# A two-layer hybrid decoder step on one NeuronCore: first K tiles in smaller chunks, operand sums of the output projection later, two retention fetches one piece sooner

## Chip, cores and metric

The kernel runs on one core of one Trainium2 chip. The metric is device microseconds of one execution, as the median of several runs; lower is better.

## What is computed

Two layers run over 520 columns: 512 prompt tokens and 8 sample tokens that share all weights. Cut to what matters:

```
h = RMSNorm(x); z = h @ W_in                       # 2048 -> 8192
conv:       y_c = B * conv3(C * xc) * silu(g)       # 1024 wide
retention:  o_n = sum_{m<=n} gamma^(n-m) (R q_n . R k_m) v_m   # 4 heads of 256
            y_r = groupnorm(o) * silu(g_ret)
x = x + concat(y_c, y_r) @ W_out                    # output projection
x = x + sigmoid(x @ W_pg) * (p @ W_ple)             # gate projection
```

A final RMSNorm follows. Outputs are x for both groups, the last two rows of the convolution's input, and the retention state.

## The kernel before

Activations lie transposed, features on partitions: 16 tiles (K tiles) of 128 x 520. All large products are done in three fp32r matmuls (`mm3`, L245): every operand is split into a high part (ScalarE, ACT, a copy that rounds) and a low part (VectorE, DVE, source minus high). Weights stream in from DRAM by SyncE (SP) in pieces of up to 128 x 512 (`load`, L220), are split (`split_w`, L225: L229 on ACT, L230 on DVE) and are used once. The 520 columns are two halves of 260, so that a product of two row tiles with two column halves can be done with seven products in place of eight (`strassen`, L290), for the first s of 16 K tiles; s is given per row pair by tables such as OUT_ROWS, and 0 means `plain` (L270). The seven products need sums of operand halves, on the weights' side (L319) and on the activations' side.

Those activation operands belong to class `Operands` (L423). Its list `todo` has one entry per K pair: split it as plain operands, and (or) sum it. `build` does the first entry: `operand_sums` (L410) makes two sum tiles by four DVE instructions of 260 columns (L413 to L416), `split` (L545: L551 on ACT, L552 on DVE, L554 and L555 where a gain is applied) splits tiles, and the source tiles are freed. Entries are built where the program calls `fill` or `need`; `fill` builds while tiles of the pair are ready and enough of the 75 tile slots are free (7 beyond the reserve for a pair that is split and summed, 3 otherwise). The first four pairs are split and summed in one go; the other pairs are split, and later loaded again and summed. For the output projection (operands `O`, L1073) the rows are 0, 8, 16, 16, 16, 16, 16, 0: the first row pair is plain, the second uses sums of four K pairs, the third of eight. Its inputs are written during the stages before: `yc` by the convolution (L1112), `ys` by retention (L1000), and are fetched by POOL's DMA queue (L1058, L1063).

At the start (L675 to L708) there is no time to stream: the four row tiles of the first two pairs are computed at once, K tiles in chunks of 1, 3, 4, 4, 4. For a chunk, SP issues a weight load for each of the four row tiles and the chunk's input tiles between them, then all are split.

Retention of a head is cut into nine pieces s0 to s8 (L1007 to L1046), which are queued and done one at a time in the middle and at the end of later row pairs (`aside`). A head's q, k, v and gate are written to DRAM and fetched again by half (256 tokens, `fetch`, L866, on POOL's queue); `send(c, "vf")` fetches the values of half c, `"gf"` the gate. A piece takes what an earlier piece has fetched.

The program is written in this order, but the order in which each engine issues is made by a list scheduler when the kernel is built (only the tail of the last layer is kept as written). Each engine then issues strictly in its order and waits on semaphores.

## Time and profile before

| | |
|---|---|
| median of 3 runs | 2168.64 us (2165.82 to 2170.73) |
| the profiled execution | 2169.1 us, span of its instructions 2167.3 us |
| PE (TensorE) busy | 2147.8 us, 99% of the span, 17861 matmuls |
| DVE (VectorE) busy | 1896.1 us, 87% |
| ACT (ScalarE) busy | 1264.5 us, 58% |
| POOL busy | 430.6 us, 20% |
| DMA | 387.31 MB, mean 179 GB/s |
| granted TensorE clock | 0.999 of full speed |

Matmuls are pipelined: a row's length runs from start to end of one matmul, and the next one starts before that end. A bracket behind a row of the timeline gives the time that the engine sat idle just before it, and which instruction's end released it.

### The profile page before, as it was taken

How to read it: one execution, taken by the hardware profiler on the slowest of the kernel's cores; microseconds unless marked ns; L12 is line 12 of the kernel's file. 1: busy time of each engine (PE TensorE's matmuls, PEld its weight loads, DVE VectorE, ACT ScalarE, POOL GpSimd, SP SyncE). 2: the span in 40 equal slices, each digit the busy share in tenths (PEclk: the TensorE clock that was granted, in tenths of full speed). 3: DMA queues.
4: the chain of work that ended last, by engine and by line, in shares of the span. 5: the costliest groups of instructions: out<-in, count | busy, mean ns of one | idle time of the engine just before them, and what ended most of it. 6: DMA issues, size and time to landing. Idle time of an engine off the chain costs nothing. (4 is left out here: it accounts for less than half of the span.)

```text
span 2167.3 us, 48178 instructions
## 1 busy us (share of the span) xinstructions
PE 2147.8 (99%) x17861; PEld 2142.1 (99%) x17861; DVE 1896.1 (87%) x3849; ACT 1264.5 (58%) x2647; POOL 430.6 (20%) x746
## 2 busy tenths in 40 slices
PE   9999999999999999999999999999999999999998
PEld 9999999999999999999999999999999999999998
DVE  8889988998999987987997988989999998879884
ACT  8656655565555655655765655565645555456565
POOL 2313222211001211200212222231111022011011
PEclk9999999999999999999999999999999999999999
DMA  8555565545543745645645566664464355566455
GB/s 288 171 175 197 181 217 184 178 157 175 158 129 118 238 156 187 215 154 160 215 144 175 172 213 191 189 209 170 151 182 149 120 158 202 176 207 200 128 164 198
DMA packets 182861, 387.31 MB, mean 179 GB/s; under 512 B 25888, under 2 KB 56352, under 8 KB 182624
## 3 DMA queue, kind: packets, MB, share of 16 engines
q1 hardware_dynamic: 128704, 212.98, 31.6%
q0 software_dynamic: 53056, 169.84, 23.8%
q8 instruction: 140, 2.29, 0.4%
q10 hardware_dynamic: 864, 1.39, 0.2%
q14 instruction: 97, 0.79, 0.1%
HBM read 318.96 MB, written 65.15 MB: 177 GB/s over the span
## 5 line engine op out<-in xcount | busy, mean ns | idle before, releaser
L247 PE MATMUL ps_g<-slot,split 128*128 128x260 f32 x5465 | 1531.6, 284 | 7.2 <-ACT slot L307 2.9
L248 PE MATMUL ps_g<-slot,split 128*128 128x260 f32 x5465 | 1534.3, 282 | 0.3 <-DVE slot L555 0.3
L249 PE MATMUL ps_g<-slot,split 128*128 128x260 f32 x5461 | 1519.9, 283 | 0.5 <-DVE split L230 0.5
L229 ACT ACTIVATE split<-raw 128x512 fp32r<-128x512 f32 (+2 forms) x1347 | 777.3, 596 | 583.1 <-DVE raw L319 213.2
L247 PEld LDWEIGHTS ps_g<-slot,split 128*128 128x128 f32 x5465 | 1024.0, 188 | 10.1 <-ACT slot L307 3.7
L248 PEld LDWEIGHTS ps_g<-slot,split 128*128 128x128 f32 x5465 | 1028.5, 188 | 0.5 <-DVE slot L555 0.5
L249 PEld LDWEIGHTS ps_g<-slot,split 128*128 128x128 f32 x5461 | 1019.8, 188 | 1.0 <-DVE split L230 1.0
L230 DVE TENSOR_TENSOR split<-raw,split 128x512 fp32r<-128x512 f32 (+2 forms) x1346 | 849.2, 652 | 172.5 <-PE ps_g L248 85.4
L319 DVE TENSOR_TENSOR raw<-raw 128x512 f32<-128x512 f32 (+1 forms) x660 | 428.9, 660 | 32.5 <-DMA raw<-wi 23.7
L307 ACT ACTIVATE slot<-ps_g 128x260 f32<-128x260 f32 x336 | 127.4, 381 | 140.6 <-PE ps_g L249 122.7
L551 ACT ACTIVATE slot<-slot 128x520 fp32r<-128x520 f32 (+1 forms) x212 | 109.2, 562 | 46.6 <-DVE slot L414 11.1
L552 DVE TENSOR_TENSOR slot<-slot,slot 128x520 fp32r<-128x520 f32 (+1 forms) x212 | 124.4, 620 | 4.1 <-ACT slot L551 3.9
L781 POOL DMA_DIRECT2D o_rets<-slot x64 | 35.3, 552 | 351.6 <-DVE slot L780 131.7
L307 DVE TENSOR_TENSOR slot<-ps_g,slot 128x260 f32<-128x260 f32 x168 | 70.9, 424 | 6.0 <-PE ps_g L249 3.7
L869 POOL DMA_DIRECT2D slot<-hs x64 | 46.2, 724 | 118.7 <-DVE split L230 42.7
L814 POOL DMA_DIRECT2D hs<-slot x64 | 35.6, 556 | 139.3 <-DVE slot L755 61.3
L780 DVE SCALAR_TENSOR_TENSOR slot<-slot,vs,slot 128x256 f32<-128x256 f32 x128 | 56.1, 481 | 4.5 <-ACT slot L776 4.3
L746 DVE TENSOR_TENSOR slot<-slot,slot 128x520 f32<-128x520 f32 x80 | 55.8, 698 | 4.7 <-DMA o_rets<-slot 3.7
L770 POOL DMA_DIRECT2D slot<-sret x64 | 35.5, 554 | 114.6 <-ACT split L229 37.3
L1058 POOL DMA_DIRECT2D slot<-x1s x76 | 40.8, 538 | 87.6 <-PE ps_g L249 27.2
L1209 POOL DMA_DIRECT2D x2s<-slot x30 | 16.4, 545 | 201.6 <-DVE slot L1204 200.6
L771 POOL DMA_DIRECT2D slot<-kq x64 | 34.9, 547 | 106.0 <-DVE slot L876 22.2
(217 smaller groups left out, 1733.8 us busy)
## 6 DMA issues: line engine op xcount, KB each, us to landing
raw<-wi SPq DMA_DIRECT2D x377, 256.0 KB, 3.9
raw<-wo SPq DMA_DIRECT2D x128, 256.0 KB, 5.4
raw<-wg SPq DMA_DIRECT2D x122, 256.0 KB, 4.1
raw<-wi SPq DMA_DIRECT2D x136, 192.0 KB, 4.0
slot<-x1s POOLq DMA_DIRECT2D x76, 260.0 KB, 5.1
slot<-sret POOLq DMA_DIRECT2D x64, 256.0 KB, 4.0
hs<-slot POOLq DMA_DIRECT2D x64, 256.0 KB, 4.0
slot<-hs POOLq DMA_DIRECT2D x64, 256.0 KB, 5.2
```

What stands on the lines that cost most here:

```text
L229: S.activation(hi, raw, AF.Copy)
L230: V.tensor_tensor(lo, raw, F(hi), SUB)
L247: PE.matmul(out, wh, xh, start=start, stop=False, skip_group_check=more)
L248: PE.matmul(out, wh, xl, start=False, stop=False, skip_group_check=more)
L249: PE.matmul(out, wl, xh, start=False, stop=stop, skip_group_check=more)
L307: fn(*args)
L319: V.tensor_tensor(out[:, n], x[:, n], y[:, n], op)
L551: keep(S.activation(hi, src[:, n], AF.Copy))
L552: V.tensor_tensor(lo, src[:, n], F(hi), SUB)
L746: V.tensor_tensor(out[:, n], v, table[:, n], MUL)
L780: keep(V.scalar_tensor_tensor(st[:, c], k, vs[:, h, e, b : b + 1], st[:, c], MUL, ADD))
L869: SIDE.dma_start(t[:, :512].rearrange("p (m n) -> p m n", m=2), src)
```

## The change

It does three things. The start's second chunk (K tiles 1 to 3) becomes two, of one and two tiles. `Operands` gets `hold`: with hold 8 (output projection alone) no pair is summed when it is split; the source tiles of the first four pairs are kept in their slots, and are summed from there after all eight pairs have been split. In retention, the gate of the first half is fetched in s2 instead of s3, the values of the second half in s4 instead of s5.

```
--- before.py
+++ after.py
@@ -62,6 +62,7 @@
 RAW = 32
 WARM = 8
 FIRST = 8
+HOLD = (8, 0, 0)
 SPLIT = 60
 
 
@@ -423,13 +424,14 @@
     class Operands:
 
 
-        def __init__(self, rows, load, reserve=0, whole=False, gain=None):
+        def __init__(self, rows, load, reserve=0, whole=False, gain=None, hold=0):
             self.rows, self.load, self.reserve, self.whole, self.gain = rows, load, reserve, whole, gain
             self.sent = []
             self.ops = [None] * KT
             self.sums = []
             self.ready = 0
-            first = max(rows[0], min(FIRST, max(rows))) // 2
+            first = max(rows[0], 0 if hold else min(FIRST, max(rows))) // 2
+            self.held = {i: None for i in range(first, hold // 2)}
             self.todo = [(True, True)] * first + [(True, False)] * (KT // 2 - first)
             self.todo = [(i, *t) for i, t in enumerate(self.todo)]
             self.todo += [(i, False, True) for i in range(first, max(rows) // 2)]
@@ -440,21 +442,28 @@
 
         def send(self):
 
-            i = self.todo[len(self.sent)][0]
-            self.sent.append([self.load(k) for k in (2 * i, 2 * i + 1)])
+            i, plain, _ = self.todo[len(self.sent)]
+            if not plain and i in self.held:
+                self.sent.append(None)
+            else:
+                self.sent.append([self.load(k) for k in (2 * i, 2 * i + 1)])
 
         def build(self):
             if not self.sent:
                 self.send()
             i, plain, summed = self.todo.pop(0)
-            f = [self.ready_tile(k, t) for k, t in zip((2 * i, 2 * i + 1), self.sent.pop(0))]
+            f = self.sent.pop(0)
+            f = self.held[i] if f is None else [self.ready_tile(k, t) for k, t in zip((2 * i, 2 * i + 1), f)]
             if summed:
                 t = operand_sums(*f)
             if plain:
                 k = 2 * i
                 halves = not self.whole and k < max(self.rows)
-                self.ops[k] = split(f[0], halves=halves, right=not halves or self.right(k))
-                self.ops[k + 1] = split(f[1])
+                keeps = i in self.held
+                self.ops[k] = split(f[0], free_src=not keeps, halves=halves, right=not halves or self.right(k))
+                self.ops[k + 1] = split(f[1], free_src=not keeps)
+                if keeps:
+                    self.held[i] = f
             else:
                 put(*f)
             if summed:
@@ -670,9 +679,9 @@
     xs = []
     X = Operands(HEADS[0][2:] + CONVS[0], from_dram(xT), gain=lambda k: norm_g(0, k))
     X.todo = [t for t in ((i, False, True) for i in range(max(X.rows) // 2))]
-    X.ready = KT // 2
+    X.ready, X.held = KT // 2, {}
     rms = Rms()
-    for a, b in ((0, 1), (1, 4), (4, 8), (8, 12), (12, 16)):
+    for a, b in ((0, 1), (1, 2), (2, 4), (4, 8), (8, 12), (12, 16)):
         raws = []
         if b == 1:
             raw = raw_ring.get(4)
@@ -1016,22 +1025,22 @@
                 scores()
                 keys()
                 values(0)
+                send(0, "gf")
 
             def s3():
                 state(0)
                 within(0)
-                send(0, "gf")
                 send(1, "qf", "kf")
 
             def s4():
                 gate(0)
                 operands()
+                send(1, "vf")
 
             def s5():
                 carried()
                 scores()
                 keys()
-                send(1, "vf")
 
             def s6():
                 values(1)
@@ -1070,7 +1079,7 @@
                 return retained(k)
             return y.pop(k) if k in y else again(yc, k - 8)
 
-        O = Operands(OUT_ROWS[l], mixer, RESERVE_OUT)
+        O = Operands(OUT_ROWS[l], mixer, RESERVE_OUT, hold=HOLD[0])
 
         SIDE.dma_start(scv, sconv[l])
         S.activation(ncv[:, :, 2:18].rearrange("p j (b r) -> p j b r", r=2)[:, :, :, 0], scv[:, :, 1, :], AF.Copy)
@@ -1126,7 +1135,7 @@
         def gate_in(k):
             return x1.pop(k) if k in x1 else again(x1s, k)
 
-        Gt = Operands(GATES[l][: (KT - tail) // 2], gate_in, RESERVE_GATE, whole=bool(tail))
+        Gt = Operands(GATES[l][: (KT - tail) // 2], gate_in, RESERVE_GATE, whole=bool(tail), hold=HOLD[1])
         for m in range(0, KT, 2):
             xs = [get(), get()]
             for i in range(2):
@@ -1171,7 +1180,7 @@
 
         X = None
         if not tail:
-            X = Operands(HEADS[l + 1] + CONVS[l + 1], next_in, RESERVE_NEXT, gain=lambda k, l=l: norm_g(l + 1, k))
+            X = Operands(HEADS[l + 1] + CONVS[l + 1], next_in, RESERVE_NEXT, gain=lambda k, l=l: norm_g(l + 1, k), hold=HOLD[2])
         for m in range(0, KT - tail, 2):
             pes, xs = [], [again(x1s, m), again(x1s, m + 1)]
             later.append(lambda m=m, w=parts(wp[l, m // 2], 0, 4), pes=pes: embed(m, w, pes))
```

The lines of the changed kernel lie further down: L230 is there L231, L307 is L308, L413 to L416 are L414 to L417, L551 and L552 are L560 and L561, L869 is L878, L1112 is L1121.

How the built order moves, at three places of layer 0. First DVE, at the entry of the output projection, from one of the two adds that end the convolution's last row pair (a PSUM bank is read into a tile) to the other; L413 to L416 and L552 are the new projection's operands. Before:

```order
L307 TENSOR_TENSOR slot_464_9225<-ps_g,slot_464_9225 128x260
L414 TENSOR_TENSOR slot_491_9458<-slot_490_9374,slot_491_9458 128x260
L552 TENSOR_TENSOR slot_509_9504<-slot_507_9498,slot_509_9504 128x260
L230 TENSOR_TENSOR split<-raw,split 128x512
L552 TENSOR_TENSOR slot_510_9505<-slot_507_9498,slot_510_9505 128x260
L552 TENSOR_TENSOR slot_512_9511<-slot_508_9501,slot_511_9510 128x520
L552 TENSOR_TENSOR slot_496_9471<-slot_490_9374,slot_495_9470 128x520
L230 TENSOR_TENSOR split<-raw,split 128x512
L552 TENSOR_TENSOR slot_476_9340<-slot_468_9320,slot_475_9339 128x520
L552 TENSOR_TENSOR slot_481_9353<-slot_477_9343,slot_481_9353 128x260
L552 TENSOR_TENSOR slot_482_9354<-slot_477_9343,slot_482_9354 128x260
L307 TENSOR_TENSOR slot_463_9224<-ps_g,slot_463_9224 128x260
```

After, from the convolution's product (L1106) on:

```order
L1106 TENSOR_TENSOR slot_458_9190<-slot_458_9190,slot_72_764 128x520
L231 TENSOR_TENSOR split<-raw,split 128x256
L416 TENSOR_TENSOR slot_504_9795<-slot_407_7009,slot_406_7007 128x260
L414 TENSOR_TENSOR slot_503_9794<-slot_406_7007 128x260
L561 TENSOR_TENSOR slot_470_9338<-slot_466_9267,slot_469_9337 128x520
L231 TENSOR_TENSOR split<-raw,split 128x512
L561 TENSOR_TENSOR slot_499_9670<-slot_498_9668,slot_499_9670 128x260
L561 TENSOR_TENSOR slot_500_9671<-slot_498_9668,slot_500_9671 128x260
L415 TENSOR_TENSOR slot_503_9794<-slot_407_7009,slot_503_9794 128x260
L231 TENSOR_TENSOR split<-raw,split 128x512 x2
L308 TENSOR_TENSOR slot_460_9227<-ps_g,slot_460_9227 128x260
L308 TENSOR_TENSOR slot_459_9226<-ps_g,slot_459_9226 128x260
```

The two adds now follow each other; the operand work that stood between them stands before or behind, and three half sums are left ahead of them.

Second ACT, a little earlier, up to the copy of one PSUM bank to another (`ps_g<-ps_g`) in the last row pair's products; L551 are splits of the output projection's operands. Before:

```order
L307 ACTIVATE slot_450_8939<-ps_g 128x260
L551 ACTIVATE slot_453_9165<-slot_406_6995 128x260
L551 ACTIVATE slot_454_9166<-slot_406_6995 128x260
L551 ACTIVATE slot_455_9171<-slot_407_6997 128x520
L551 ACTIVATE slot_457_9175<-slot_451_9159 128x520
L551 ACTIVATE slot_459_9179<-slot_452_9160 128x520
L229 ACTIVATE split<-raw 128x512
L229 ACTIVATE split<-raw 128x384
L307 ACTIVATE ps_g<-ps_g 128x260
```

After (L1073 writes sample columns into retention's tiles):

```order
L1073 ACTIVATE slot_472_9344<-gs 128x8
L230 ACTIVATE split<-raw 128x384
L230 ACTIVATE split<-raw 128x512
L230 ACTIVATE split<-raw 128x384
L560 ACTIVATE slot_473_9347<-slot_471_9341 128x260
L230 ACTIVATE split<-raw 128x512
L560 ACTIVATE slot_474_9348<-slot_471_9341 128x260
L560 ACTIVATE slot_475_9353<-slot_472_9344 128x520
L308 ACTIVATE ps_g<-ps_g 128x260
```

The five splits in a row ahead of the copy are three, with weight splits between them, and of other pairs.

Third POOL's DMA queue, around the values of the last head's second half (`slot_394_6588` before, `slot_385_6411` after). Before:

```order
L770 DMA slot_379_6321<-sret 128x512
L771 DMA slot_380_6322<-kq 128x512
L983 TENSOR_TENSOR rstp<-rstd,half_neg 128x2
L781 DMA o_rets<-slot_359_5983 128x512
L1000 DMA ys<-slot_376_6280 128x2x256
L1112 DMA yc<-slot_369_6091 128x520
L869 DMA slot_394_6588<-hs 128x2x256
L770 DMA slot_395_6625<-sret 128x512
L771 DMA slot_396_6626<-kq 128x512
```

After:

```order
L779 DMA slot_379_6333<-sret 128x512
L780 DMA slot_380_6334<-kq 128x512
L790 DMA o_rets<-slot_359_5995 128x512
L992 TENSOR_TENSOR rstp<-rstd,half_neg 128x2
L1009 DMA ys<-slot_368_6098 128x2x256
L878 DMA slot_385_6411<-hs 128x2x256
L1121 DMA yc<-slot_370_6105 128x520
L779 DMA slot_395_6637<-sret 128x512
L780 DMA slot_396_6638<-kq 128x512
```

The fetch moved ahead of the store of a convolution tile (`yc`) and stands behind a retention store only.

## Rows read from the trace of the kernel before

**Rows 1.** The page: busy time by engine, and one group of matmuls.
```profile
PE 2147.8 (99%) x17861; PEld 2142.1 (99%) x17861; DVE 1896.1 (87%) x3849; ACT 1264.5 (58%) x2647; POOL 430.6 (20%) x746
...
L247 PE MATMUL ps_g<-slot,split 128*128 128x260 f32 x5465 | 1531.6, 284 | 7.2 <-ACT slot L307 2.9
```

**Rows 2.** Windows: stretch, busy us and instructions by engine, clock, DMA share, GB/s.
```profile
0.00:20.00 20.00, 17.73 (x121) 17.02 (x122) 12.02 (x22) 13.21 (x24) 11.19 (x28) 1.00 0.85 288
200.00:300.00 100.00, 100.00 (x838) 100.00 (x837) 90.86 (x202) 60.91 (x134) 27.57 (x47) 1.00 0.63 193
700.00:720.00 20.00, 18.80 (x157) 18.60 (x157) 20.00 (x44) 15.00 (x41) 7.28 (x14) 1.00 0.71 220
720.00:730.00 10.00, 7.88 (x64) 7.47 (x63) 10.00 (x22) 9.87 (x28) 3.29 (x7) 1.00 1.01 376
730.00:760.00 30.00, 30.00 (x253) 29.98 (x252) 26.57 (x55) 13.61 (x29) 6.55 (x13) 1.00 0.62 185
```
The engines are PE, PEld (weight load), DVE, ACT, POOL.

**Rows 3.** Timeline of PE: start, length, instruction, idle before and its releaser.
```profile
9.75 0.51 PE L247 MATMUL ps_g<-slot,split 128*128 128x260 f32 x2 [0.64 <-ACT slot L554]
10.54 0.39 PE L248 MATMUL ps_g<-slot,split 128*128 128x260 f32 x1 [0.29 <-DVE slot L555]
...
23.29 0.39 PE L247 MATMUL ps_r<-slot,split 128*128 128x260 f32 x1 [0.49 <-ACT split L229]
...
491.60 0.63 PE L913 MATMUL ps_vt<-ident,slot 128*128 128x128 f32 x4 [0.94 <-DMA slot<-hs]
...
706.46 0.39 PE L247 MATMUL ps_g<-slot,split 128*128 128x260 f32 x1 [1.20 <-ACT ps_g L307]
...
726.13 0.39 PE L247 MATMUL ps_g<-slot,split 128*128 128x260 f32 x1 [0.83 <-ACT slot L307]
...
729.26 0.39 PE L247 MATMUL ps_g<-slot,split 128*128 128x260 f32 x1 [1.29 <-ACT split L229]
...
1118.85 0.39 PE L247 MATMUL ps_g<-slot,split 128*128 128x260 f32 x1 [0.40 <-ACT ps_g L307]
...
1471.65 0.39 PE L248 MATMUL ps_st<-slot,slot 128*128 128x256 f32 x1 [0.46 <-DVE slot L918]
...
1787.85 0.39 PE L247 MATMUL ps_g<-slot,split 128*128 128x260 f32 x1 [1.29 <-ACT slot L307]
...
1795.74 0.39 PE L247 MATMUL ps_g<-slot,split 128*128 128x260 f32 x1 [0.56 <-ACT slot L307]
```

**Rows 4.** Timeline of DVE at the entry of layer 0's output projection.
```profile
710.01 0.75 DVE L1092 SCALAR_TENSOR_TENSOR slot<-slot,vec,slot 128x511 f32<-128x511 f32 x1
...
710.80 0.70 DVE L230 TENSOR_TENSOR split<-raw,split 128x512 fp32r<-128x512 f32 x1
711.41 0.43 DVE L415 TENSOR_TENSOR slot<-slot,slot 128x260 f32<-128x260 f32 x1
...
726.98 0.45 DVE L307 TENSOR_TENSOR slot<-ps_g,slot 128x260 f32<-128x260 f32 x1
727.32 1.94 DVE L552 TENSOR_TENSOR slot<-slot,slot 128x520 fp32r<-128x520 f32 x3
729.15 0.45 DVE L416 TENSOR_TENSOR slot<-slot,slot 128x260 f32<-128x260 f32 x1
```

**Rows 5.** Timeline of POOL: the fetch of the last head's second values.
```profile
484.07 0.57 POOL L1112 DMA_DIRECT2D yc<-slot  x1 [9.59 <-DVE slot L746]
484.64 0.73 POOL L869 DMA_DIRECT2D slot<-hs  x1
```

**Rows 6.** Timeline of SP's queue: the first weight load of the second chunk.
```profile
2.86 0.44 SPq L222 DMA_DIRECT2D raw<-wi  x1
```

**Rows 7.** DMA issues from 0 to 14 us: count, KB each, median us to landing.
```profile
raw<-wi SPq DMA_DIRECT2D x4, 192.0 KB, 5.9
...
ident<-ident_d SPq DMA_DIRECT2D x1, 64.0 KB, 5.6
```

**Rows 8.** Waits of SP's queue from 0 to 26 us: total, times, longest.
```profile
SPq L222 <- DMA raw<-wi: 4.7, 6, 1.4
```

More of the change, by code (lines that the diff above doesn't have):

```diff
@@ L423, in trunk_kernel, with __init__ @@
     class Operands:
-        def __init__(self, rows, load, reserve=0, whole=False, gain=None):
+        def __init__(self, rows, load, reserve=0, whole=False, gain=None, hold=0):
             self.rows, self.load, self.reserve, self.whole, self.gain = rows, load, reserve, whole, gain
@@ L431, in __init__ @@
             self.ready = 0
-            first = max(rows[0], min(FIRST, max(rows))) // 2
+            first = max(rows[0], 0 if hold else min(FIRST, max(rows))) // 2
+            self.held = {i: None for i in range(first, hold // 2)}
             self.todo = [(True, True)] * first + [(True, False)] * (KT // 2 - first)
@@ L441, in send @@
         def send(self):
-            i = self.todo[len(self.sent)][0]
-            self.sent.append([self.load(k) for k in (2 * i, 2 * i + 1)])
+            i, plain, _ = self.todo[len(self.sent)]
+            if not plain and i in self.held:
+                self.sent.append(None)
+            else:
+                self.sent.append([self.load(k) for k in (2 * i, 2 * i + 1)])
         def build(self):
@@ L449, in build @@
             i, plain, summed = self.todo.pop(0)
-            f = [self.ready_tile(k, t) for k, t in zip((2 * i, 2 * i + 1), self.sent.pop(0))]
+            f = self.sent.pop(0)
+            f = self.held[i] if f is None else [self.ready_tile(k, t) for k, t in zip((2 * i, 2 * i + 1), f)]
             if summed:
@@ L455, in build @@
                 halves = not self.whole and k < max(self.rows)
-                self.ops[k] = split(f[0], halves=halves, right=not halves or self.right(k))
-                self.ops[k + 1] = split(f[1])
+                keeps = i in self.held
+                self.ops[k] = split(f[0], free_src=not keeps, halves=halves, right=not halves or self.right(k))
+                self.ops[k + 1] = split(f[1], free_src=not keeps)
+                if keeps:
+                    self.held[i] = f
             else:
@@ L672, in trunk_kernel @@
     X.todo = [t for t in ((i, False, True) for i in range(max(X.rows) // 2))]
-    X.ready = KT // 2
+    X.ready, X.held = KT // 2, {}
     rms = Rms()
-    for a, b in ((0, 1), (1, 4), (4, 8), (8, 12), (12, 16)):
+    for a, b in ((0, 1), (1, 2), (2, 4), (4, 8), (8, 12), (12, 16)):
         raws = []
@@ L1173, in trunk_kernel @@
         if not tail:
-            X = Operands(HEADS[l + 1] + CONVS[l + 1], next_in, RESERVE_NEXT, gain=lambda k, l=l: norm_g(l + 1, k))
+            X = Operands(HEADS[l + 1] + CONVS[l + 1], next_in, RESERVE_NEXT, gain=lambda k, l=l: norm_g(l + 1, k), hold=HOLD[2])
         for m in range(0, KT - tail, 2):
```

9 lines of the change are left out of this document (5 added, 4 removed).

## Prediction

> **What bounds the kernel now.** I read the page's busy times first: TensorE (PE) is busy 2147.8 of the 2167.3 us span [rows 1]. The next, VectorE (DVE), stands at 1896.1. So two things can change the time: PE's work, and PE's pauses. The change leaves PE's work alone (the built program has as many PE instructions, of the same shapes), so the question is which of the 19.5 us of idle PE go away and which new ones come. What a pause costs needs the pace: in a stretch without pauses PE starts 838 matmuls in 100 us [rows 2], one every 0.12 us, while the row of one lasts 0.28 us [rows 1], since matmuls overlap. A pause therefore costs the idle time in its bracket plus 0.16 us.
>
> Next I went along PE's timeline and kept the waits that end on another engine [rows 3]; the reader is to see where they bunch. Idle plus 0.16, they make four groups. Start: 0.80 and 0.45 us at 9.75 and 10.54 (second K tile, its split not there), 0.65 at 23.29 (weight split). Retention: 1.10 at 491.60 (values fetched from DRAM) and 0.62 at 1471.65 (VectorE's low part of the transposed values). Entry of the output projection, layer 0: 1.36, 0.99 and 1.45 at 706.46, 726.13 and 729.26; layer 1: 1.45 and 0.72 at 1787.85 and 1795.74. Untouched by the change: 0.56 at 1118.85.
>
> The entries are the largest group, 5.97 us. There DVE is busy 30.00 of 30 us from 700 to 730, ScalarE (ACT) 9.87 of the last 10, and the DMA engines have a share of 1.01 in those 10 [rows 2]. PE waits four times for ACT's copy that empties a PSUM bank, once for a weight split. The copies are late because operand splits stand before them in ACT's queue, which wait for DVE and loads in turn.
>
> **The change, part by part.**
>
> *Sums later in the output projection.* Before, each of the first four K pairs is split and at once summed: four half sums (L413 to L416), then two splits of sum tiles. The projection's first row pair uses plain products and reads no sums; the second is the first to read them. After, all eight pairs are split first. DVE and ACT do the same instructions; nothing is added. The steps from one start to the next are 0.79 us for a convolution tap with the eight-column one behind it, 0.61 for a 512-column split, 0.34 for 260 elements, and (729.15 - 727.32)/3 = 0.61 for 520 [rows 4]. Per layer 4 x (4 x 0.34 + 2 x 0.61) = 10.3 us of DVE move. How much of it stood ahead of PE's waits, the order tells. From the last convolution's first tap (L1092) to the second of DVE's two bank-emptying adds (L307), layer 0, the trace has 726.98 - 710.01 = 16.97 us without a gap. In the changed order 25 instructions stand there: six 512-column splits, two of 256 (taken as 0.34 each), six splits, three half sums and an add of 260 elements, two splits and a product of 520, two taps with their eight-column ones. That is 3.7 + 0.7 + 3.4 + 1.8 + 1.6 = 11.2 us: 5.8 us less, over twice the 0.99 + 1.45 us that PE lost in this stretch. Ten instructions between the two adds become none. On ACT, five operand splits in a row before the copy that PE awaited at 706.46 become three, of which two are short. I therefore take the four copy waits as gone: 1.36 + 0.99 + 1.45 + 0.72 = 4.5 us. The 1.45 us for a weight split I leave standing: bytes loaded are the same, and where the DMA share is 1.01 no weight has a reason to land sooner. Bounds: 0 and 5.97.
>
> The moved work lands after row pair 0. From 730 to 760 DVE has 30 - 26.57 = 3.4 us free [rows 2], and 5.8 us were freed just before: 9.2 us for 10.3. Nearly covered; if that cover goes, rival 3 has the price. New tight places I price at 0.9 us in all, 0.45 a layer, near the shortest old wait between neighbours, 0.56 at 1118.85 [rows 3]. Held source tiles keep eight slots longer, but a pair now asks for four free slots fewer before it is split: cost nothing, as the loads in POOL's order come earlier, not later.
>
> *Retention fetches.* The wait at 491.60 is for the second chunk's values. POOL issued that fetch at 484.64, behind a store that had held POOL's queue for 9.59 us, and PE could go on 7.0 us after the issue [rows 5]. Now the fetch stands ahead of that store. Gain 1.10 us, bounds 0 and 1.10. The gates also come a piece sooner; no PE wait in the trace is for them. The 0.62 at 1471.65 is an accident of order in the same step; I count half, 0.3, bounds 0 and 0.62.
>
> *First K tiles.* The chunk of three K tiles becomes one and two. Four loads of 192 KB become four of 64 and four of 128. SP issues four more (0.44 us each [rows 6]); ACT and DVE make four more splits, while busy 13.21 and 12.02 of the first 20 us [rows 2]. Bytes stay. The 192 KB loads landed after a median of 5.9 us, the 64 KB one of the identity, issued just before them, after 5.6 [rows 7]: a smaller load alone buys 0.3 us, and not having two more tiles' weights ahead of tile 1's buys the rest, at most the 1.25 us of the first two waits. But the wait at 23.29 is for a later weight, with the DMA engines 0.85 busy over these 20 us, and takes part of it back. I take 0.5 us; bounds a loss of 1.5 (rival 2) and a gain of 1.25.
>
> A rule of the Trainium skill speaks against this part: "DMA: Bandwidth & Descriptors", section "Bandwidth", asks for transfers of 1 MiB and has one of 64 KB at 0.95 us, 138 GB/s. An estimate from that page: tile 1's weights one by one would take 4 x 0.95 = 3.8 us, against 0.9 us at the trace's rate, the start would lose 2.9 us, and the sum would be -2.1 us. The trace does not agree: 288 GB/s over the first 20 us.
>
> *Sum.* -4.5 + 0.9 - 1.1 - 0.3 - 0.5 = -5.5 us. The profiled execution took 2169.1 us, which gives 2163.6; the median of the runs, 2168.64, is 0.46 lower, so I forecast 2163.1 us.
>
> **The rivals.**
> 1. *The loads decide, not VectorE.* Copies come in time, but operand and weight loads queue and PE waits for late splits instead. For: the share of 1.01, and the wait at 729.26 is of that kind. Against: loads of the first pairs move forward and spread. Half of the 4.5 us comes back: -3.2, 2165.4 us. Chance 0.22.
> 2. *The start loses.* SP's four issues delay every later weight by 4 x 0.44 = 1.8 us and the wait at 23.29 grows by that less 0.3: -5.5 + 0.5 + 1.5 = -3.5, 2165.1 us. For: SP issues without pause at first. Against: soon SP itself waits for loads to land, 4.7 us in six waits [rows 8]. The Trainium skill's rule on small transfers, named above, would act here. Chance 0.09.
> 3. *Slower: the sums come late.* If none of the 5.8 us freed before 730 is usable, because DVE waits there for operands, 10.3 us of sums meet 3.4 us of free DVE before row pair 1 reads them: PE waits 6.9 us in each layer, -5.5 + 13.8, 2176.9 us. It decides where DVE idles over 5.8 us up to 730, without which nothing is late. Against: no gap there before, and operands now load earlier. Chance 0.05.
> 4. *The order gives it back.* The scheduler moves instructions everywhere, and as many pauses come as go: 2168.6 us. Chance 0.10.
>
> **How the numbers follow.** The forecast has 0.54. A measurement of this kernel tells 0.2%, 4.3 us, from no change; the border is 2164.3, and the forecast lies 1.2 us beyond it. Low end: start (1.25), retention (1.72) and entries (5.97) all gained and nothing lost, 2168.64 - 8.94 = 2159.7, taken as 2159.5. High end: rivals 1, 2 and most of 4, 2168.5. Left out are rival 3 and the rest. Faster: the forecast and a little of rivals 1 and 2, 0.56; same: those rivals and 4, 0.38; slower: rival 3 and a little, 0.06.
>
> **What would show it.** Right: no pause at the second value transposes of layer 0's last head; no waits for ACT's copies at both entries; hardly a sum operation between DVE's two adds; less free DVE from 730 to 760; PE's second K tile about 1 us sooner, the wait near 23 us longer. Wrong: pauses for splits or operand tiles between 715 and 730 (rival 1), or for sum tiles in the 30 us after the entry (rival 3).

## The result, and the profile after

| | before | after |
|---|---|---|
| median, 20 runs each on one chip | 2169.16 us (2165.82 to 2172.57) | 2172.91 us (2168.87 to 2182.76) |
| ratio | | 1.0020 [1.0014, 1.0027] |
| the profiled execution, its span | 2169.1, 2167.3 us | 2171.1, 2169.3 us |

The change costs 4.3 us (0.0020 x 2169). The forecast was 2163.1 us, a gain of 5.5; the time lies above the range, on the other side of no change.

The page after, beside [rows 1]:

```profile
PE 2149.2 (99%) x17861; PEld 2142.8 (99%) x17861; DVE 1897.7 (87%) x3853; ACT 1266.4 (58%) x2651; POOL 432.4 (20%) x746
...
L248 PE MATMUL ps_g<-slot,split 128*128 128x260 f32 x5465 | 1533.6, 284 | 9.5 <-ACT split L230 5.3
```

PE does the same 17861 matmuls. In the costliest group its idle time went from 7.2 to 9.5 us, and the engine behind most of it is no longer ACT's bank copy (L307, now L308) but ACT's weight split (L230). Idle time moved and grew. Where, PE's timeline after shows, beside [rows 3]:

```profile
19.86 0.51 PE L248 MATMUL ps_g<-slot,split 128*128 128x260 f32 x2 [0.28 <-ACT slot L563]
21.84 0.39 PE L248 MATMUL ps_g<-slot,split 128*128 128x260 f32 x1 [1.00 <-ACT split L230]
...
712.18 0.39 PE L248 MATMUL ps_g<-slot,split 128*128 128x260 f32 x1 [1.44 <-ACT split L230]
721.25 0.39 PE L248 MATMUL ps_g<-slot,split 128*128 128x260 f32 x1 [1.23 <-ACT split L230]
...
1223.38 0.39 PE L248 MATMUL ps_g<-slot,split 128*128 128x260 f32 x1 [1.56 <-ACT ps_g L308]
...
1783.97 0.39 PE L248 MATMUL ps_g<-slot,split 128*128 128x260 f32 x1 [1.14 <-ACT split L230]
1786.14 0.39 PE L248 MATMUL ps_g<-slot,split 128*128 128x260 f32 x1 [0.46 <-ACT split L230]
...
2122.01 0.39 PE L248 MATMUL ps_g<-slot,split 128*128 128x260 f32 x1 [1.08 <-ACT slot L308]
```

Each wait that the forecast named is gone (9.75, 10.54, 491.60, 1471.65, the copy waits at 706.46, 726.13, 1787.85 and 1795.74), and nearly every stretch has a new one. All pauses of the two profiles, each counted as the part of the step from one matmul's start to the next that exceeds 0.12 us, where that part is over 0.18 us:

| stretch of the program | before, us | after, us |
|---|---|---|
| start, to 30 us | 2.93 | 2.65 |
| 30 to 700 (layer 0's retention lies here) | 1.72 | 0.82 |
| entry of the output projection, layer 0 | 3.80 | 3.23 |
| about 1080 to 1200 | 1.18 | 1.83 |
| layer 1, about 1200 to 1775 | 1.90 | 3.14 |
| entry of the output projection, layer 1 | 2.18 | 2.21 |
| the rest, to the end | 1.52 | 2.48 |
| sum | 15.2 | 16.4 |

The sum grew by 1.1 us. PE's last matmul came 2.70 us later than before; the other 1.6 us are steps slightly longer than 0.12 us, none a pause. One profile of each kernel thus shows 2.0 us of span where the medians differ by 4.3: single rows vary between executions, and the parts had to be priced by timed runs.

The entry of layer 0, windows after (columns as in [rows 2]):

```profile
700.00:710.00 10.00, 10.00 (x86) 10.00 (x85) 9.01 (x19) 7.01 (x20) 4.15 (x8) 1.00 0.56 163
710.00:720.00 10.00, 8.56 (x67) 8.00 (x65) 7.14 (x16) 4.76 (x15) 2.74 (x6) 1.00 1.00 356
720.00:730.00 10.00, 8.77 (x73) 8.75 (x73) 10.00 (x24) 9.05 (x24) 2.66 (x5) 1.00 0.79 252
730.00:760.00 30.00, 29.92 (x249) 29.71 (x249) 28.62 (x59) 14.00 (x29) 5.94 (x12) 1.00 0.64 199
```

The ten us from 710 before:

```profile
710.00:720.00 10.00, 10.00 (x86) 10.00 (x85) 10.00 (x25) 6.16 (x20) 3.54 (x7) 1.00 0.89 293
```

DVE, full from 700 to 730 before, is free for 0.99 and 2.86 us up to 720. Yet PE, which ran through 710 to 720 before, now loses 1.44 us there. It waits for ACT, and ACT for DMA (timeline of ACT after):

```profile
708.93 0.73 ACT L560 ACTIVATE slot<-slot 128x260 fp32r<-128x260 f32 x2 [1.72 <-DMA slot<-yc]
...
711.50 0.63 ACT L230 ACTIVATE split<-raw 128x512 fp32r<-128x512 f32 x1 [1.32 <-DMA raw<-wo]
...
718.91 0.63 ACT L230 ACTIVATE split<-raw 128x512 fp32r<-128x512 f32 x1 [3.92 <-DMA raw<-wo]
```

DMA is fully busy (share 1.00, before 0.89). Loads of one kind took longer, by the DMA issues from 695 to 720 (columns as in [rows 7]), first before, then after:

```profile
raw<-wo SPq DMA_DIRECT2D x10, 256.0 KB, 6.0
```

```profile
raw<-wo SPq DMA_DIRECT2D x9, 256.0 KB, 7.1
```

POOL issues two loads of `xT` at this point, which it issued at 721.6 and 723.7 before (timeline of POOL after):

```profile
709.05 0.54 POOL L1142 DMA_DIRECT2D slot<-xT  x1 [1.25 <-PE ps_g L249]
709.58 0.54 POOL L1067 DMA_DIRECT2D slot<-yc  x1
710.10 0.54 POOL L1142 DMA_DIRECT2D slot<-xT  x1
710.63 1.59 POOL L1072 DMA_DIRECT2D slot<-ys  x3
```

That is rival 1's picture: the loads, not VectorE, decide once VectorE has time.

### The profile page after: what moved, and what is told of

It is laid out like the page before. It is cut to its first block, busy times and chain, and to the rows that moved or that the text cites. A ratio compares the mean times of both kernels' runs of the same rounds, so it can differ in the third digit from the quotient of the medians.

```text
span 2169.3 us, 48205 instructions
## 1 busy us (share of the span) xinstructions
PE 2149.2 (99%) x17861; PEld 2142.8 (99%) x17861; DVE 1897.7 (87%) x3853; ACT 1266.4 (58%) x2651; POOL 432.4 (20%) x746
## 5 line engine op out<-in xcount | busy, mean ns | idle before, releaser
L230 ACT ACTIVATE split<-raw 128x512 fp32r<-128x512 f32 (+2 forms) x1351 | 778.8, 595 | 595.9 <-PE ps_g L250 213.0
L231 DVE TENSOR_TENSOR split<-raw,split 128x512 fp32r<-128x512 f32 (+2 forms) x1350 | 847.0, 647 | 165.1 <-PE ps_g L249 76.3
L308 ACT ACTIVATE slot<-ps_g 128x260 f32<-128x260 f32 x336 | 127.4, 381 | 125.8 <-PE ps_g L250 113.8
L560 ACT ACTIVATE slot<-slot 128x520 fp32r<-128x520 f32 (+1 forms) x212 | 109.7, 563 | 41.0 <-DVE slot L415 9.7
L561 DVE TENSOR_TENSOR slot<-slot,slot 128x520 fp32r<-128x520 f32 (+1 forms) x212 | 124.2, 613 | 4.5 <-ACT slot L560 3.8
L308 DVE TENSOR_TENSOR slot<-ps_g,slot 128x260 f32<-128x260 f32 x168 | 70.8, 422 | 5.6 <-PE ps_g L250 5.3
L878 POOL DMA_DIRECT2D slot<-hs x64 | 46.2, 723 | 146.1 <-DVE split L231 31.6
```

The source lines that it names most:

```text
L230: S.activation(hi, raw, AF.Copy)
L231: V.tensor_tensor(lo, raw, F(hi), SUB)
L308: fn(*args)
L560: keep(S.activation(hi, src[:, n], AF.Copy))
L561: V.tensor_tensor(lo, src[:, n], F(hi), SUB)
L878: SIDE.dma_start(t[:, :512].rearrange("p (m n) -> p m n", m=2), src)
```

## The experiments

Three theories run through the experiments. **Parts**: each of the three edits has a price of its own, and they add. **O**: the scheduler moves instructions everywhere, and the loss comes from the order as a whole. **L**: at the entries, loads issued in a burst make the weights late. Later runs add **G** (the moved gate fetch costs, not the values), layer 1 as the place of the loss, and the addresses of the tile slots.

A comparison of the built orders answers part of O without a run: the chunk edit changes only the first 5% or so of the program, holding only the two output projections, the two fetches together only the retention stretches, and the changed kernel is the three added up. So O in its wide form is false. (One run below is an exception: with the values alone moved, the order at the entry of layer 0's output projection changes too.)

The edits are undone one by one from the changed kernel. *Without hold*:

```
-HOLD = (8, 0, 0)
+HOLD = (0, 0, 0)
```

*Without chunks*:

```
-    for a, b in ((0, 1), (1, 2), (2, 4), (4, 8), (8, 12), (12, 16)):
+    for a, b in ((0, 1), (1, 4), (4, 8), (8, 12), (12, 16)):
```

*Gate back* (s2, s3) and *values back* (s4, s5):

```
                 values(0)
-                send(0, "gf")
...
                 within(0)
+                send(0, "gf")
...
                 operands()
-                send(1, "vf")
...
                 keys()
+                send(1, "vf")
```

Each ratio is to runs of the kernel before on the same chip, timed together with it. "The n-th matmul" is a place in the program: the same count in each kernel.

**The change again.** No edit.

> The changed kernel once more, unedited, for a second profile. If the stalls are set by the order, those of 1.0 us and more at 710.5, 719.8, 1221.5, 1782.6 stand again at the same matmuls, each within 0.5 us. If they are set by how long single transfers take in that execution, half of them or more differ by over 0.5 us or are gone, and others stand elsewhere. The stall of 1.24 us at 2120.6, where a store and a load through DRAM are waited for, I expect to differ. Time 2173, 0.2% above before.

1.0024 [1.0013, 1.0035]: it is slower again. The four pauses stand at the same matmuls. Three differ by 0.42 us or less; the one near 1221 grew from 1.56 to 2.99 us of idle, so the order sets the place and not always the size.

**Hold alone.** Without chunks, gate and values back.

> The kernel before with the hold alone (hold 8 at the output projection; start and retention as before). Theory L (loads take the place of VectorE at the projection's entry, and this is what the change costs): at both entries TensorE waits for weight splits (L230) instead of copies, 2.5 to 4 us per layer, so the entries give nothing back and this kernel alone is slower than before by 2 to 4 us, about 2172. Theory O (order: ScalarE and VectorE stand in another order all over the program, and stalls come and go at places that the change does not name): entries as in the changed kernel, stalls outside them differ from before's from 700 us on and not before it; time anywhere within 3 us of before. The forecast's own claim, 3.6 us faster (4.5 less 0.9), has both theories against it.

1.0004 [0.9995, 1.0013], no gain. The copy waits are gone and three weight-split waits stand in their place (timeline of PE):

```profile
712.13 0.39 PE L248 MATMUL ps_g<-slot,split 128*128 128x260 f32 x1 [0.40 <-ACT split L230]
713.55 0.39 PE L248 MATMUL ps_g<-slot,split 128*128 128x260 f32 x1 [0.92 <-ACT split L230]
...
722.28 0.39 PE L248 MATMUL ps_g<-slot,split 128*128 128x260 f32 x1 [0.81 <-ACT split L230]
```

Against before, PE gains 0.84 us over the entry (from the 5800th matmul, at 702 us, to the 6000th) and loses 0.77 in the 500 matmuls behind it, of which a pause explains 0.22.

**Start alone.** Without hold, gate and values back.

> The kernel before with the start's chunks 1, 1, 2, 4 alone. Theory L: only the first 30 us differ; 0.3 us faster there (the changed kernel's profile has 1.6 us of stalls there against 1.9), no stall elsewhere changes by over 0.3 us, time 2169 within 1 us. Theory O: the stalls at 491, 706 to 729, 1788 to 1796 come out otherwise or go, and new ones of 0.5 to 2 us stand at other places after 100 us; time differs from before by 1 to 4 us either way although nothing after the first 25 us was edited.

1.0005 [0.9996, 1.0013]. The 42nd matmul (the second K tile) comes 1.36 us sooner, the 145th 0.58 us later than before. The gain is given back at K tiles 4 to 7 (timeline of PE):

```profile
17.07 0.39 PE L248 MATMUL ps_g<-slot,split 128*128 128x260 f32 x1 [0.27 <-ACT slot L563]
19.07 0.39 PE L248 MATMUL ps_g<-slot,split 128*128 128x260 f32 x1 [0.28 <-ACT split L230]
21.15 0.51 PE L248 MATMUL ps_g<-slot,split 128*128 128x260 f32 x2 [1.10 <-ACT slot L563]
```

In the first 14 us the 64 and 128 KB loads landed after 4.2 and 4.3 us (the 192 KB loads of before: 5.9), and the first five 256 KB loads after 8.4 (before, the first six: 7.2); over 20 us the DMA engines moved 273 GB/s (before: 288). The first weights gain and the next ones lose. That the bytes bound the input here is argued, not shown.

**Retention alone.** Without hold and chunks.

> The kernel before with the two retention fetches one piece sooner, alone. Both theories: the stall at 491 (1.10 us) is gone. Theory L: nothing else changes, 2168, 1.1 us faster. Theory O: the gain at 491 is there, and stalls of 0.5 to 2 us come or go outside retention (entries of the projection, convolution, tail); time anywhere from 2 us faster to 4 us slower than before.

1.0006 [0.9997, 1.0015]. The pause at 491 is gone, but there are new ones in layer 1, near 1220 us (below), and near 2120.

**Gate alone, values alone.** As retention alone, with values back in the first and gate back in the second.

> The kernel before with only the fetch of the first half's gate moved up a piece. Theory G: a stall of 1.7 to 3.2 us at matmul 10082 (1220 us), with VectorE's wait for a store to DRAM at 1205 to 1209 ahead of it, the stall at 491 still there (0.6 to 1.1 us), TensorE 2 to 3 us later between matmuls 10000 and 10300 than before, time 1.5 to 3 us over before. Rival V: the stall there is half as large as in the changed kernel or absent.

> The kernel before with only the fetch of the second half's values moved up a piece. Theory G (what retention loses comes from the gate's fetch: in layer 1's first head it stands in POOL's queue between two stores of queries and keys, whose slots ScalarE and VectorE wait for): the stall at 491 (1.10 us) is gone, none over 0.5 us at matmul 10082 (1220 us), time 0.5 to 1.5 us under before. Rival V (any sooner fetch there loads the DMA engines and makes weights late): a stall of 1 us or more within 1200 to 1250 us here too.

1.0013 [1.0004, 1.0022] and 1.0011 [1.0003, 1.0020]. Theory G holds in one half: the pause near 1220 does not appear without the moved gate. The rest of it fails. This profile of the gate alone has neither the pause near 1220 nor the one at 491, both of which G expected, and the values alone are slower than before instead of faster. The values alone are no clean part of the change either: ACT's and DVE's order also differs from before's from 645 to 776 us, at the entry of layer 0's output projection, which the two fetches together leave as it was. PE pauses there, where before had its copy waits (timeline of PE, values alone):

```profile
722.01 0.39 PE L248 MATMUL ps_g<-slot,split 128*128 128x260 f32 x1 [1.91 <-ACT slot L308]
```

**Two parts of three.** *Undo hold* (without hold), *undo retention* (gate and values back), *undo start* (without chunks).

> The changed kernel without the hold (start and retention kept). The copy waits at 704, 725 and 1794 are back, the waits for weight splits at matmuls 5874, 5935 and 14746 are gone. By the profiles the hold moved TensorE's arrival from matmul 4100 to 6500 by +0.4 us and from 14700 to 15500 by +0.4 us: without it 0.8 us under the changed kernel, 2172, and slower than before by 0.1 to 0.2%. By the forecast's step it would be 3.6 us over the changed kernel.

> The changed kernel with retention as before (hold and start kept). If retention's gate is the largest part of the loss: 2.5 us under the changed kernel, about 2170.3, no stall at matmul 10082, the stall at 491 back. If the loss is spread evenly: 1.3 us under it, 2171.5.

> The changed kernel with the start's chunks as before (hold and retention kept). If each part adds its own: 1.0010 of before, 2170.7, and 1.5 us under the changed kernel. If the loss lies in the retention part's collision in layer 1 alone (2.6 us at matmul 10082 in five of five profiles with both fetches moved, one of them to come here): a stall of 1.7 to 3.2 us there again and 1.0015 to 1.002, 2172.

1.0006 [0.9997, 1.0015], 1.0006 [0.9997, 1.0015] and 1.0019 [1.0010, 1.0028]. With the start undone nearly the whole loss is there; with hold or retention undone most of it is gone, 3.0 us in either case, where 0.8 was expected of the hold and 2.5 or 1.3 of retention. With retention undone the pause at 491 was expected back and did not come. At layer 0's entry the start undone has the weight-split waits again:

```profile
711.04 0.39 PE L248 MATMUL ps_g<-slot,split 128*128 128x260 f32 x1 [1.30 <-ACT split L230]
721.02 0.39 PE L248 MATMUL ps_g<-slot,split 128*128 128x260 f32 x1 [2.10 <-ACT split L230]
```

**Control.** All three undone, with the new code still in place.

> The changed kernel's file with all three parts undone: the same instructions in the same order as the kernel before. It shows what two equal programs differ by. If the comparison is even: ratio 1.000 within 0.0009, so that the ratios of 1.0004 to 1.0013 of the parts stand. If kernels that are timed beside before come out slow by themselves: 1.0005 to 1.001, and the parts alone cost nothing. Its profile shows the stalls at matmuls 39, 141, 4039, 5821, 5976, 5989, 14789 and 14848; those that stand in it and in before's within 0.3 us are the order's, the others the execution's.

1.0002 [0.9993, 1.0011]. The instructions are those of before; still its profile has pauses that before's has not (1.34 us at the 10531st matmul, 0.89 at the 11387th). Single pauses of about a microsecond in one profile are no evidence for a part.

**Loads later at the entry.** Hold alone, and

```
-RESERVE_OUT = 8
+RESERVE_OUT = 12
```

> The hold alone with 12 instead of 8 free slots kept back when the output projection's operands are built, so that fewer operand loads are sent at once. Theory L (a burst of loads at the projection's entry makes weights land late): the two loads of the layer's input that stood among the operands' loads come later, the weight-split stalls at matmuls 5872, 5874 and 5935 (0.56, 1.07 and 0.98 us with the hold alone) lose half or more, 1 to 1.5 us over both layers; time 2168, at or under before. Rival: the stalls stay, since what is late is the convolution's own rows that the first operands need; then it is as the hold alone, 1.0004 of before.

1.0005 [0.9996, 1.0014]. The waits stayed:

```profile
711.71 0.39 PE L248 MATMUL ps_g<-slot,split 128*128 128x260 f32 x1 [1.18 <-ACT split L230]
720.92 0.39 PE L248 MATMUL ps_g<-slot,split 128*128 128x260 f32 x1 [1.33 <-ACT split L230]
```

L's expectation failed. The edit moved only the second of the two `xT` loads, and that by less than 2 us (713.04 us, 711.41 with the hold alone), and the weights landed after 7.6 us (before 6.0), so it is a weak trial of L. The lateness itself is no accident of one profile: by the DMA issues from 695 to 720 the `wo` loads landed after a median of 6.9 to 8.0 us in the seven profiles that hold layer 0 as the change does, and after 5.8 to 7.1 in the eleven that do not hold it. That the late weights are what PE waits for is shown; that the burst makes them late is argued.

**More slots for a held pair.** Hold alone, and

```
-  ... >= reserve + (7 if plain and summed else 3):
+  ... >= reserve + (7 if plain and (summed or i in self.held) else 3):
```

> The hold alone, but a held pair asks for 7 free slots beyond the reserve, as a summed pair did before, not 3. Theory L: operand loads and splits go out later and the entry's stalls turn from weight splits back towards splits of operands, with DVE freer than before; entries 2 to 3 us of stall in layer 0, time within 1 us of the hold alone. Rival (the lower slot demand is what frees the entry): the copy waits of before (1.36, 0.99) come back.

1.0009 [1.0000, 1.0018], no better. A copy wait came back (0.99 us of idle at 705.94); the `xT` loads came later (712.16 and 713.22), the weights landed after 6.3 us, and layer 0's entry had only 1.55 us of pauses, as L would have it. Yet PE still lost time up to the 6500th matmul, and layer 1 had 3.86.

**Hold in layer 1 alone.** Without chunks, gate and values back, and

```
-        O = Operands(OUT_ROWS[l], mixer, RESERVE_OUT, hold=HOLD[0])
+        O = Operands(OUT_ROWS[l], mixer, RESERVE_OUT, hold=HOLD[0] if l else 0)
```

> The kernel before with the hold in layer 1 only. By the mean of the profiles so far the hold costs layer 0 1.1 us (0.5 up to matmul 6000, 0.6 from there to 6500) and layer 1 nothing (0.1): equal to before within 0.0009, waits for weight splits at matmuls 14744 to 14748 in place of the copy waits at 14789 and 14848, and TensorE's way from matmul 14600 to 15500 within 0.5 us of before's.

1.0003 [0.9993, 1.0012]. Its profile lost 4.0 us between the 14500th and the 15500th matmul, which was not expected; the median did not. The loss behind layer 0's entry, from the 6000th to the 6500th matmul, is not there (0.00 us against before); it is 0.48 to 0.77 us in all seven profiles that hold layer 0 as the change does, though undo hold and values alone lose as much there, at single pauses elsewhere.

**The gate again.** Gate alone, once more.

> The gate's fetch alone once more. In five profiles with both fetches moved the stall at matmul 10082 was the time by which one weight load (128x256) landed after TensorE was there, plus 0.65 us: 1.07 to 1.15 late and 1.72 to 1.81 us of stall, 2.50 late and 3.15; with the gate alone the load landed 0.60 us early and there was no stall. The same rule holds here: lateness plus 0.65 us, within 0.1. If values sooner are needed for the stall, there is none however late the load lands. The stall at 17540 stands, 0.7 to 1.2 us.

1.0012 [1.0003, 1.0021]. The first profile of this program had no pause at the 10082nd matmul; this one has 3.24 us of idle. The two rows on ACT (split of a 128x256 weight, then the bank copy that PE awaits), and SP's issue of that weight, first gate alone:

```profile
1218.03 0.42 ACT L230 ACTIVATE split<-raw 128x256 fp32r<-128x256 f32 x1 [1.82 <-DMA raw<-wi]
1218.36 0.37 ACT L308 ACTIVATE ps_g<-ps_g 128x260 f32<-128x260 f32 x1
...
1215.46 0.33 SPq L223 DMA_DIRECT2D raw<-wi  x1
```

then the gate again:

```profile
1223.16 0.42 ACT L230 ACTIVATE split<-raw 128x256 fp32r<-128x256 f32 x1 [4.51 <-DMA raw<-wi]
1223.48 0.37 ACT L308 ACTIVATE ps_g<-ps_g 128x260 f32<-128x260 f32 x1
...
1218.04 0.33 SPq L223 DMA_DIRECT2D raw<-wi  x1
```

One program: the load is issued 2.6 us later, and its split starts 2.57 us behind the issue in the one and 5.12 in the other. ACT goes in order; the copy behind the split is late with it, and PE waits for the copy. In before the copy stands ahead (timeline of ACT):

```profile
1218.81 0.37 ACT L307 ACTIVATE ps_g<-ps_g 128x260 f32<-128x260 f32 x1 [0.27 <-PE ps_g L249]
...
1221.10 0.83 ACT L229 ACTIVATE split<-raw 128x256 fp32r<-128x256 f32 x2 [1.29 <-DMA raw<-wi]
```

so that a late weight costs nothing there. In the control this load landed 1.13 us behind PE's arrival at that matmul, and PE did not pause. In the seven profiles that pause there, all with the gate moved in layer 1, the load lands 1.07 to 2.76 us behind PE's arrival, and each pause is that lateness plus 0.65 us, as expected. The pause in the tail stands too, smaller than expected (0.39 us).

**Fetches sooner in layer 0 only.** First alone (without hold and chunks), then within the changed kernel:

```
                 values(0)
-                send(0, "gf")
+                if l == 0:
+                    send(0, "gf")
...
                 within(0)
+                if l:
+                    send(0, "gf")
```

and the values in the same way.

> The kernel before with both fetches sooner in layer 0 only. If the retention part loses in layer 1 alone: no stall at matmul 10082 and none over 0.3 us at 17540, the stall at 491 gone, and 1.0 of before within 0.0009 (2168 to 2169). If the stall at 17540 comes from the gate in layer 0 too (other slots for all that follows): it stands here, 0.7 to 1.2 us.

> The changed kernel with the two fetches sooner in layer 0 only (hold and start kept). If layer 1's fetches carry the retention part's loss (2.6 to 5.2 us at matmul 10082, 1 us at 17540, less 1 to 1.5 us won between matmuls 11000 and 12500): 1.0008 to 1.0012 of before, 2 to 3 us under the changed kernel. If hold and start carry it: 1.0018 or more.

1.0013 [1.0004, 1.0022] and 1.0026 [1.0015, 1.0037]: the loss stays though layer 1's fetches are as before and the pause near 1220 is gone. That pause is real, but retention's price does not hang on it. Two others stay. One is in the tail, at 2123.98 (idle 1.37). The other is at the 10199th matmul, and with it PE still loses 1.31 and 2.25 us between the 10000th and the 10300th matmul (timeline of PE, the first of the two runs):

```profile
1235.12 0.39 PE L250 MATMUL ps_g<-slot,split 128*128 128x260 f32 x1 [0.91 <-DVE split L231]
```

It stands in eight of the ten profiles with the gate moved in either layer, and in none of the ten others. In the first of these runs every engine's instructions, their order and the semaphores that they wait for are those of before from 570 us on.

**Other addresses.** The kernel before, and the changed one, with the 75 tile slots laid out and handed out in other orders:

```
-        self.free = list(range(n))
+        self.free = [37 * i % n for i in range(n)]
+        for i in range(n):
+            pool.tile([P, T], F32, tag=f"s{i}", name=f"first{i}")
```

> The kernel before with the 75 tile slots laid out in memory in another order (slot number 37 i modulo 75 is the i-th taken); every engine's instructions, their order and their waits are the same. Theory A (addresses set the loss of the kernels with moved fetches): the time moves by 0.05% or more from before, or stalls of 0.7 us and more appear at matmuls 10199 or 17540. Rival (addresses are nothing): 1.000 within 0.0009 and no stall there.

> The changed kernel with the slots laid out in that other order, nothing else. Theory A: the stalls at matmuls 10199 (0.6 to 0.8 us) and 17540 (1.25 and 1.55 us) are gone or differ by over 0.5 us, time 1 us or more away from the changed kernel's 2173. Rival: both stand, and the stall at 10082 is again the lateness of one weight load plus 0.65 us; 1.0020 to 1.0025 of before.

1.0006 [0.9997, 1.0015] and 1.0021 [1.0010, 1.0032]. Addresses don't make the loss, nor the tail's pause: none in the first, 0.95 us in the second. (The first ratio allows up to 0.15% for the addresses themselves.)

**What a pause costs when the clock falls.** The rows of pauses leave one thing out. In nine of the twenty profiles the granted TensorE clock falls from 2.4 to 1.2 GHz before the last 10 us of the program, ten times in all, each time for 3.4 us. Each time PE had just paused, or was still pausing, for 1.28 to 3.24 us. The gate again, from 0.7 us behind its pause of 3.24 us at 1223.90, and the 3.4 us after that (columns as in [rows 2]):

```profile
1224.60:1228.00 3.40, 3.40 (x18) 3.40 (x17) 1.55 (x4) 3.28 (x8) 0.00 (x0) 0.50 0.37 97
1228.00:1231.40 3.40, 3.40 (x31) 3.40 (x30) 3.05 (x9) 1.31 (x3) 0.59 (x1) 1.00 0.56 170
```

PE works on 18 matmuls in the first and on 31 in the second. The 13 that are missing are 1.6 us at 0.12 us each, an estimate of what this pause cost beyond its idle time plus 0.16. It came behind the long pauses near 1220 us of the gate again and the change again (2.99 us), and behind the pause of the values alone at 722. Other pauses as long were followed by no fall (2.70 us near 1224, the changed kernel with other addresses), and the profiles before and after have none, so it is no part of the table above. It is a smaller part of the loss: where an execution's mean clock was 0.999, the changed kernel took 2172.0 us on average (14 of its 27 executions) and before 2168.7 (101 of the 145 timed beside the variants). So about 3.3 us of the loss stand where the clock hardly fell.

**The parts put together.** A least-squares fit of the 19 ratios (these 18 and the result) to three prices, each of them present or not: hold 1.5 us (95%: 0.8 either way), chunks 0.5 (1.0), any fetch moved 2.4 (0.7). The sum is 4.4 us, measured 4.3; the squared residuals are 9.9 for 16 degrees of freedom, so prices that add are consistent with all the runs. One price stands for one fetch moved or both: the gate's and the values' do not add. Kernels timed together share the runs of before, so the errors are rough.

No version beats the kernel before: undo retention had the same median as before (2168.45 and 2168.43 us), and hold in layer 1 alone is within its interval.

## Why the prediction was wrong

Numbers in brackets behind a price are its 95% error from the fit.

**Hold: -4.5 + 0.9 us forecast, +1.5 (0.8) found.** Right: VectorE was full and is not now, the four copy waits went (0.28 us of one is left in layer 1), the sums moved behind the entry, and DVE's free time from 730 to 760 fell, from 3.4 to 1.4 us. Rival 3 did not come; PE is busy 29.92 of these 30 us. The step that failed is "bytes loaded are the same, and where the DMA share is 1.01 no weight has a reason to land sooner". It asked whether weights would land sooner, not whether they would land later. Bytes were the same, but not when they were asked for: POOL issued the two `xT` loads 12 to 14 us sooner, and `wo` landed after 7.1 us in place of 6.0. Of the operand loads the prediction even said that they come earlier, and priced that at nothing: "cost nothing, as the loads in POOL's order come earlier, not later". The sum took each wait gone as time gained; in their place came waits for the next late input. In layer 0 the working said 1.36 + 0.99 - 0.45 = 1.90 us, for the two copy waits there; the third pause, 1.45 us for a weight split, it left standing, and that one went too. After gained 0.53 us from the 5800th matmul to the 6000th (late by -0.93 there, by -1.46 here) and lost 0.68 up to the 6500th, mostly in steps without a pause: nothing is left of it. Rival 1 had the mechanism, but gave back half.

**Retention: -1.4 us forecast, +2.4 (0.7) found.** Two steps failed. First, the size of the gain: the pause at 491 is gone in all eleven profiles with a fetch moved in layer 0, but in nine profiles without it is 1.10, 1.04, 1.03, 0.84, 0.62, 0.29, 0.19, 0 and 0 us, 0.57 on average. The 1.10 of before was the largest of them, and taken as its price. Two of the eleven moved the gate alone, so the values' place in the queue is not all that removes it. The 0.62 at 1471.65, of which it counted half, was such a draw too: in two other profiles of before's instructions (control, other addresses of before) it does not stand. Second, "the gates also come a piece sooner; no PE wait in the trace is for them" counted a moved DMA at nothing. It is not free on its queue (timeline of POOL after):

```profile
1204.84 0.54 POOL L823 DMA_DIRECT2D hs<-slot  x1 [7.63 <-DVE slot L766]
1205.40 0.72 POOL L878 DMA_DIRECT2D slot<-hs  x1
1206.12 0.56 POOL L780 DMA_DIRECT2D slot<-kq  x1
1206.67 0.55 POOL L823 DMA_DIRECT2D hs<-slot  x1
```

The gate's fetch stands between two stores of the next head. The second store goes out later, DVE and ACT wait for its end (after, DVE, then ACT; the first wait was 0 before, the second 2.08):

```profile
1208.84 0.69 DVE L885 TENSOR_TENSOR slot<-slot,slot 128x512 fp32r<-128x512 f32 x1 [1.36 <-DMA hs<-slot]
```

```profile
1211.42 0.48 ACT L926 ACTIVATE slot<-ps_kt,vec 128x256 fp32r<-128x256 f32 x1 [3.38 <-DMA hs<-slot]
```

SP's next weight buffer comes free later (longest wait of SP's queue for DVE from 1203 to 1224, 13.7 us, before 12.6), the weight lands later, and ACT, with its split now in front, holds up the copy:

```profile
1222.63 0.42 ACT L230 ACTIVATE split<-raw 128x256 fp32r<-128x256 f32 x1 [3.52 <-DMA raw<-wi]
1222.96 0.37 ACT L308 ACTIVATE ps_g<-ps_g 128x260 f32<-128x260 f32 x1
```

By the matmul counts PE loses 2.6 us from the 10000th to the 10300th in after, retention alone among others, and 0 within 0.1 us in kernels whose gate stays. But the layer 0 runs are as slow without this pause, and lose 1.31 and 2.25 us in the same stretch at another one. So it is one way of losing and not the sum.

The pause in the tail, near 2120 us at the 17540th matmul, is in all ten profiles with the gate moved in either layer (0.39 to 1.55 us) and in none of the ten others. The instructions there, their order and their waits are the same. What differs is when POOL asks for the third `x2s` tile: 5.41 to 7.04 us after the store before it in the ten, 2.83 to 3.69 in the others (after; before, POOL had waited 2.28 there and ACT 1.15):

```profile
2113.00 0.54 POOL L1067 DMA_DIRECT2D slot<-x2s  x1 [4.88 <-ACT split L230]
...
2118.14 0.30 ACT L1273 ACTIVATE slot<-slot,vec 128x8 f32<-128x8 f32 x1 [3.68 <-DMA slot<-x2s]
```

Why a fetch moved a thousand us earlier, even in layer 0 alone, does this is open. So is what the values' fetch alone costs: it has neither pause and was 1.0011, but it changed the order at layer 0's entry as well.

**First K tiles: -0.5 us forecast, +0.5 (1.0) found.** The working was right up to its last step: the second K tile came 1.48 us sooner, and a later wait took it back, all of it rather than more than half. Within the error the two sizes can't be told apart. The loss of 2.9 us that the Trainium skill's page "DMA: Bandwidth & Descriptors" ("Bandwidth") would give by its 0.95 us for 64 KB, a figure for transfers that GpSimd (POOL) issues, is not there: the second K tile came sooner, and start alone is +1.1 us, from -0.9 to +2.8.

**The price of a pause.** Idle plus 0.16 us holds only while the clock stays: in the gate again it was short by an estimated 1.6 us.

**The rivals.** Rival 1's picture fits, more strongly than priced. Rival 2's give-back acted as a small loss. Rival 4 said that as many pauses come as go, which is close (15.2 and 16.4 us), but for another reason than it gave: the order is unchanged outside the start, the two entries and the retention stretches. The one rival on the slower side was not the one that came; a moved DMA issue as a cause of loss was not among them.

## What to carry to other kernels

When PE is 99% busy, an idle time in its timeline is what the last input was late, not what removing it gains: look for the second-latest input and when its load is issued once the first is out of the way. Price a moved DMA at the place it goes to: whose store or load stands behind it on its queue, and which in-order engine has a copy for PE queued behind the one who waits for that. A pause read from one execution is one draw; before building a gain on 1 us, see it in several executions. Behind a long pause, read the granted clock too: its fall can add over a microsecond.

## What the runs showed of the hardware

- The landing time of one and the same 128 KB weight load differed by a factor of two between executions of one program: its split began 2.57 and 5.12 us behind its issue (gate alone, the gate again).
- Executions of identical instructions differ by 1 us and more at single matmuls (1.10, 1.04 and 0 us at 491 in before, the control and other addresses of before), while the medians agree: control 1.0002 [0.9993, 1.0011].
- Other addresses of all tile slots changed nothing measurable (1.0006 [0.9997, 1.0015]).
- The granted TensorE clock fell from 2.4 to 1.2 GHz for 3.4 us behind pauses of PE of 1.28 us and more, ten times in twenty profiles, though not behind every such pause; 18 matmuls in place of 31 (the gate again).
